# Moving two scan steps and one small product, repeating 17 scan matmuls, and five warm-ups less, in a retention and HGRN2 decoder step

## The chip, the cores and the metric

The kernel runs on one core of a Trainium2 chip. The metric is the device time of one execution in microseconds, of which there are three runs of the kernel before and one profiled execution. TensorE (PE in the profile) does the matrix products, with its weight loads shown apart as PEld; VectorE (DVE), ScalarE (ACT) and GpSimd (POOL) do the rest, and SyncE (SP) issues most transfers.

## The reference

One layer of a hybrid decoder: the normalised input is projected to eight groups of 512 columns, half of which feed four heads of retention (fixed decay by head) and half four heads of HGRN2 (a learned forget gate for each column); the gated outputs go through one output projection.

In short form:

```python
h = rmsnorm(x, norm_g)
p = (h @ w_in).astype(jnp.float32)
rq, rk, rv, rg, hq, hf, hi, hgate = jnp.split(p, 8, axis=-1)
rq, rk = rotary(rq, pos), rotary(rk, pos) * RET_DK ** -0.5
o_ret, s_ret = chunked_decay_recurrence(rq, rk, rv, log_gamma, s_ret)   # S = f*S + k v^T, o = S^T q
o_ret = head_rmsnorm(o_ret, ret_g) * silu(rg)
logf = logaddexp(log(lb), log1p(-lb) + log_sigmoid(hf))
kin = (1 - lb) * sigmoid(-hf)
o_hg, s_hg = chunked_decay_recurrence(silu(hq), kin, hi, logf, s_hg)
o_hg = head_rmsnorm(o_hg, hg_g) * silu(hgate)
y = x + concatenate([o_ret, o_hg]) @ w_out
```

It does so for a prompt of 2048 tokens of width 1024 and for eight single new tokens with states of their own (the "decode" rows). Everything is float32.

## The kernel before, in words

**Units and products.** The input projection is cut into 24 units, u = 0 to 23, in the repeating order H (HGRN2's f and q of one head), G (the gates) and R (retention's k and q of one head). Units 0 to 11 work on the first half of the prompt, 12 to 23 on the second. Eight units of the output projection follow, and the V products stand ahead of all. Each unit is a Strassen-Winograd product of seven block products; a block product is 12 matmuls of 128x512, since an operand is split into a high and a low part (names ending in h and l) in order to keep float32 accuracy. The results carry names like aG, eR, bR: the unit's kind is the second letter.

**The order.** The table AT gives nearly every piece of work a position in units of one block product, seven to a unit. Pieces are put in a heap (`at`, and `after` for a position relative to the running one) and written out in that order. The order that comes out is the order of every engine: nothing is rearranged later. The scan of the head with index u//3 gets its positions from `AT["hgrn"]` plus an offset from `AT["hd"][u // 3]`, one row of four for each of the eight scans (here counted from one: the second scan belongs to u = 3, the fourth to u = 9).

**The scan.** An HGRN2 head is scanned in steps s0 to s3, which stand between the block products of later units. Step s0 (`scores0`) makes 32 diagonal matmuls (L1287) and 32 of `small` (L1269). Steps s1 and s2 (`scores`) each make 32 calls of `small` on kept copies, tile plh<-fh,qh, and 32 on the running k and q, plh<-qth,kh. Step s3 makes 16 calls at L1321 and 16 at L1330. A float32 call is two passes on TensorE, each with a weight load, so the trace counts 64 for 32 calls. Between two steps ScalarE copies k and half of q to the kept tiles (`keep`, L1248 and L1249), VectorE multiplies running k and q by the products of the forget gates (`update`, L1234 and L1237, tiles kh and qth), and then puts the scores into place (`put`, COPY_PREDICATED). The first half of a step waits for the copies, the second for the update.

**Other names.** `dec_mm` (L809) makes the projection of the eight decode rows for unit u: 16 calls into tile pdp, from the weight tiles r6A, r6S and so on of that unit. `dec_copy` takes it off. potr is a transpose by TensorE. L750 is the addition that combines block products on VectorE (kr<-bR,kr). At the start TensorE makes 7 calls of 128x128 and `AT["wu"]` calls of 32x8 on a tile of ones (L237 and L240) before the first product.

Of the kernel before, what the change touches and what calls it, by code (L numbers as in the profile page):

```python
# [19 lines left out]
P = 128  # L20
# [6 lines left out]
CH = HALF // P  # L27
# [21 lines left out]
def spooled(u):  # L49
    return u % 3 != 1 and u % 12 != 11  # L50
# [3 lines left out]
AT = {'wvl': (0.55, 0.6, 6.2, 6.6),  # L54
 's2': (0.4, 2.6),
 'vd': (9.4, 11.2),
 'hgrn': {'s0': 12.1,
          's1': 15.8,
          's2': 17.6,
          'load': 17.5,  # L60
          's3': 19.7,
          'k': 20.9,
# [63 lines left out]
 'x1s': (0.5, 1.8, 1.9, 3.4, 5.0),  # L126
 'wo': (26.9, 71.0, 101.8, 122.8),
 'wos': (0.0, 2.3, 3.3),
 'wu': 35,
 'wop': (140.0, 2.133, 2.1, 2.833),  # L130
 'gate': {'G': 0.95, 'store': 1.6, 'R': 0.8, 'H': 0.7, 'root': 0.5, 'scale': 1.15, 'gt': 1.2, 'tr': 0.6},
 'fin': 1.0,
# [9 lines left out]
         'fin': 25.2},  # L142
 'dh': ((12.15, 14.75), (17.55, 20.15), (27.15, 28.65)),
 'dhs': (-5.0, -2.2, -2.2, -1.5),
 'hd': ((0.0, 0.0, 0.0, 0.0), (0.0, 0.0, -0.5, -0.5), (0.0, 0.0, 0.0, 0.0), (0.3, 0.0, 0.0, 0.0),
        (0.0, 0.0, 0.0, 0.0), (0.0, 0.5, 0.0, 0.0), (0.0, 0.0, 0.0, 0.0), (0.0, 0.0, 0.0, 0.5)),
 'retL': {'load': 12.0,
          's': 11.55,
# [37 lines left out]
def step_kernel(ctx, tc, a, out):  # L186
    nc = tc.nc
    pe, act, dve, pool, sp = nc.tensor, nc.scalar, nc.vector, nc.gpsimd, nc.sync
# [29 lines left out]
    def at(pos, f):  # L218
        count[0] += 1
        heapq.heappush(ev, (pos, count[0], f))  # L220

    def after(d, f):
        at(now[0] + d, f)
# [11 lines left out]
    wu = ps_tr.tile([P, P], F32, tag="tr", name="wu")  # L235
# [535 lines left out]
    def w_load(u, n):  # L771
        R[u, n] = t_get([P, GW], f"r{u}{n}")
        row, kh = {"A11": (0, 0), "S3": (1, 0), "A22": (1, 1), "A12": (0, 1)}[n]
        sp.dma_start(R[u, n].rearrange("p (k t) -> p k t", k=4), w_src(u, row, kh))

    def w_s1(u):
        R[u, "S1"] = t_get([P, GW], f"r{u}S1")
        w_add(u, "S1", "S3", "A22", ALU.add)

    def w_s3(u):  # L780
        w_add(u, "S3", "A11", "S3", ALU.subtract)

    def w_s2(u):
        R[u, "S2"] = t_get([P, GW], f"r{u}S2")
        w_add(u, "S2", "A22", "S3", ALU.subtract)

    def w_s4(u):
        R[u, "S4"] = t_get([P, GW], f"r{u}S4")
        w_add(u, "S4", "A12", "S2", ALU.subtract)

    def w_split(u, n):
        w = W[u, n] = r_get(f"w{u}{n}")
        split_raw(w, R[u, n])
        t_done(R[u, n])
        if u < 12 and spooled(u):
            after(AT["late"], lambda: pool.dma_start(w_dram[u][W_NAMES.index(n)], w.bitcast(F32)))

    def w_reload(u, n):
        w = W[u, n] = r_get(f"w{u}{n}")
        sp.dma_start(w.bitcast(F32), w_dram[u - 12][W_NAMES.index(n)])  # L800
# [3 lines left out]
    def dec_mm(u):  # L804
        dec["pt"] = ps_o.tile([P, P], F32, tag="o", name=f"pdp{u}")
        for j in range(4):
            for g, n in enumerate(("A11", "A12", "S3", "A22")):
                at_ = 32 * (4 * (g % 2) + j)
                pe.matmul(  # L809
                    dec["pt"][32 * g : 32 * g + 32], xz[:, at_ : at_ + 32], R[u, n][:, j * P : (j + 1) * P],  # L810
                    start=(j == 0), stop=(j == 3),
                )

    def dec_copy(u):
        dec["e"] = t_get([P, P], f"de{u}")
        act.activation(dec["e"], dec["pt"], AF.Copy)

    def dec_sel(u):
        pt = ps_o.tile([P, 2, NB], F32, tag="o", name=f"pds{u}")
        pe.matmul(pt, dec["e"], sel16, start=True, stop=True)  # L820
        t_done(dec["e"])
        act.activation(draw[:, u % 3, :, u // 3], pt, AF.Copy)

    def prep_events(u):
        U = 7 * u
        w, d = AT["w"], AT["dec"]
        if 12 <= u < 24 and spooled(u):
            for name in W_NAMES:
                at(U + AT["re"][name], lambda name=name: w_reload(u, name))
            return  # L830
        for n, name in enumerate(("A11", "S3", "A22", "A12")):
            at(U + {0: -7.6, 1: -8.6}.get(u, AT["w24"][0] if u == 24 else w["load"] if u % 3 or u >= 12 else w["load0"]) + 0.5 * n, lambda name=name: w_load(u, name))
        if u < 12:
            if u == 3:
                at(AT["hgrn"]["s2"] + AT["hd"][0][2] + 0.01, lambda: dec_mm(u))
            else:
                at(U + d["mm" if u % 3 or not u else "mm0"], lambda: dec_mm(u))
            at(U + (-0.65 if u < 2 else d["copy" if u % 3 else "copy0"]), lambda: dec_copy(u))
            at(U + d["sel"], lambda: dec_sel(u))
        if u == 24:  # L840
            w = dict(w, **dict(zip(("S1", "S3", "S2", "S4"), AT["w24"][1:])))
        at(U + w["S1"], lambda: w_s1(u))
        at(U + w["S3"], lambda: w_s3(u))
        at(U + w["A11"], lambda: w_split(u, "A11"))
        at(U + w["S2"], lambda: w_s2(u))
        at(U + w["sS1"], lambda: w_split(u, "S1"))
        at(U + w["S4"], lambda: w_s4(u))
        at(U + w["sS2"], lambda: w_split(u, "S2"))
        at(U + w["sS4"], lambda: w_split(u, "S4"))
        at(U + w["sA12"], lambda: w_split(u, "A12"))  # L850
        at(U + w["sS3"], lambda: w_split(u, "S3"))
        at(U + w["sA22"], lambda: w_split(u, "A22"))
# [349 lines left out]
    def hgrn_rec(u):  # L1202
        half, h = u // 12, (u % 12) // 3
        name = f"h{half}{h}"
        hd = NH + h
        d = units[u]
        f, k, q, qt = d["f"], d["k"], d["q"], d["qt"]
        box = {}

        def views(b):  # L1210
            return (
                qt.rearrange("p (n two b) -> p n two b", two=2, b=b),
                k.rearrange("p (n two b) -> p n two b", two=2, b=b),
            )
# [7 lines left out]
        def products(lo, hi):  # L1222
            if lo == 0:
                box["fp"] = s_ctx["up"].tile([P, HALF], F32, tag="fp", name=f"fp{name}")
            for li in range(lo, hi):
                two = spans(li).rearrange("p (n two) -> p n two", two=2)
                dve.tensor_tensor(spans(li + 1), two[:, :, 0], two[:, :, 1], op=ALU.mult)

        def update(li):
            b = LEVELS[li]  # L1230
            qv, kv = views(b)
            nb = HALF // (2 * b)
            two = spans(li).rearrange("p (n two) -> p n two", two=2)
            dve.tensor_tensor(  # L1234
                kv[:, :, 0, :], kv[:, :, 0, :], two[:, :, 1:2].to_broadcast([P, nb, b]), op=ALU.mult
            )
            dve.tensor_tensor(  # L1237
                qv[:, :, 1, :], qv[:, :, 1, :], two[:, :, 0:1].to_broadcast([P, nb, b]), op=ALU.mult
            )

        kept_k, kept_q = q, f[:, :512]
# [11 lines left out]
            after(0.35, copies)  # L1253
            after(1.1, lambda: update(li))

        def small(dst, li, kept=False):
            b = LEVELS[li]
            m = 32 // (2 * b)
            for c in range(CH):
                for i in range(4):  # L1260
                    at_ = c * P + 32 * i
                    if not kept:
                        kk = k[:, at_ : at_ + 32]
                        n0 = (c * 4 + i) * m
                        qq = views(b)[0][:, n0 : n0 + m, 1, :]
                    else:
                        kk = kept_k[:, at_ : at_ + 32]
                        qq = kept_q[:, at_ // 2 : at_ // 2 + 16]
                    pe.matmul(dst[32 * i : 32 * i + 32, c], kk, qq, start=True, stop=True)  # L1269

        def put(src, li):
            b = LEVELS[li]
# [8 lines left out]
        def scores0():  # L1281
            pa = ps_lv.tile([P, 2, CH, 32], F32, tag="lv", name=f"pa{name}")
            pd, p0 = pa[:, 0], pa[:, 1, :, :16]
            for c in range(CH):
                for i in range(4):
                    cc = slice(c * P + 32 * i, c * P + 32 * i + 32)
                    pe.matmul(pd[32 * i : 32 * i + 32, c], k[:, cc], q[:, cc], start=True, stop=True)  # L1287
            small(p0, 0)
            update(0)
            products(0, 1)  # L1290
            keep(1)

            def diagonal():
                products(1, len(LEVELS))
                dve.tensor_tensor(Ab, pd, id32.unsqueeze(1).to_broadcast([P, CH, 32]), op=ALU.mult)
                put(p0, 0)

            after(0.6, diagonal)

        def scores(li):  # L1300
            pl = ps_lv.tile([P, 2, CH, 16], F32, tag="lv", name=f"pl{name}{li}")
            small(pl[:, 0], li, True)
            small(pl[:, 1], li + 1)
            update(li + 1)
            keep(li + 2)

            def puts():
                put(pl[:, 0], li)
                put(pl[:, 1], li + 1)

            after(0.1, puts)
# [524 lines left out]
    for hd in range(8):  # L1836
        mm, sel = AT["dh"][hd % 3]
        p0 = 84 + 21 * (hd // 3)
# [116 lines left out]
```

## Time and profile before

| | us |
|---|---|
| median of three runs | 995.23 |
| lowest and highest | 995.17, 996.35 |
| profiled execution, its own time | 994.56 |
| its span | 992.8 |
| TensorE busy | 978.9 (99%) |
| VectorE busy | 779.6 (79%) |
| ScalarE busy | 575.5 (58%) |
| GpSimd busy | 252.5 (25%) |

The profile is of one execution. The difference between its own time and its span, 1.76 us, is what lies around the first and last recorded instruction. Busy time counts an instruction from its start to its end; TensorE's ends are modelled, and its instructions overlap, so the start times of neighbours tell better than the durations what one instruction costs. An idle time stands in brackets behind the instruction that it precedes, with what ended it; "issue" there means that nothing in the profile was waited for. Over the whole span the granted clock of TensorE is 0.999 of full speed. The DMA engines are 50 to 99% busy in most slices, since the weights, the prompt and the spooled intermediate tiles come and go all the time.

### The profile page before, as it was taken

The page shows a single profiled execution, that of the slowest core. Times are in us where ns is not written, and L with a number is a line of the kernel's source. Part 1 is how long each engine was busy: PE and PEld are TensorE (multiplying, and loading weights), DVE is VectorE, ACT ScalarE, POOL GpSimd, SP SyncE. Part 2 cuts the span into 40 slices and gives each one's busy share as a digit, 9 for nine tenths or more (in the row PEclk, how much of TensorE's full clock was granted, in tenths as well). Part 3 has the DMA queues.
Part 4 walks back from the last instruction along what each step waited for, and adds up shares of the span by engine and source line. Part 5 has one row for each costly group of instructions (what it writes and reads, how often), then busy time and mean ns, then how long its engine had stood idle before and what let it go on. Part 6 is the DMA issues. An engine that isn't in the chain of part 4 may idle for free. (4 is left out here: it accounts for less than half of the span.)

```text
span 992.8 us, 22960 instructions
## 1 busy us (share of the span) xinstructions
PE 978.9 (99%) x8831; PEld 815.9 (82%) x8831; DVE 779.6 (79%) x1355; ACT 575.5 (58%) x1348; POOL 252.5 (25%) x404
## 2 busy tenths in 40 slices
PE   9999999999999999999999999999999999999997
PEld 7788888888878887888888888888888878878886
DVE  6967696888778888878898766877867799867774
ACT  7855524856656664765885555456467577524332
POOL 1421231111332342232022222222237202312121
PEclk9999999999999999999999999999999999999999
DMA  9756669748868987784986993994996497784522
GB/s 310 239 182 245 223 218 360 291 154 301 261 194 279 300 284 266 269 273 159 354 277 187 320 307 121 317 303 130 317 333 215 156 362 275 244 267 156 212 85 85
DMA packets 121820, 244.05 MB, mean 246 GB/s; under 512 B 12600, under 2 KB 53184, under 8 KB 119024
## 3 DMA queue, kind: packets, MB, share of 16 engines
q1 hardware_dynamic: 98544, 164.69, 50.9%
q0 software_dynamic: 22880, 77.65, 21.1%
q8 instruction: 69, 1.13, 0.5%
q14 instruction: 39, 0.32, 0.1%
q10 hardware_dynamic: 288, 0.27, 0.1%
HBM read 155.97 MB, written 89.72 MB: 247 GB/s over the span
## 5 line engine op out<-in xcount | busy, mean ns | idle before, releaser
L1248 ACT ACTIVATE qh<-kh 128x1024 f32<-128x1024 f32 x24 | 25.5, 1062 | 46.3 <-DVE kh L1234 46.2
L1671 ACT ACTIVATE yj<-xro 128x512 f32<-128x512 f32 (+1 forms) x25 | 15.6, 624 | 60.3 <-DVE xro L750 42.7
L1234 DVE TENSOR_TENSOR kh<-kh,fph 128x512 f32<-128x512 f32 x48 | 33.0, 687 | 13.6 <-PE plh L1269 10.9
L1128 ACT ACTIVATE obh<-poh 128x128 f32<-128x128 f32 x64 | 16.9, 290 | 29.3 <-PE poh L1124 29.3
L1237 DVE TENSOR_TENSOR qth<-qth,fph 128x512 f32<-128x512 f32 x48 | 32.8, 683 | 0.0
L1128 ACT ACTIVATE obr<-por 128x128 f32<-128x128 f32 x64 | 16.8, 276 | 27.1 <-PE por L1124 27.1
L373 POOL TENSOR_TENSOR ms<-ms 128x2 f32<-128x2 f32 x8 | 10.0, 1255 | 86.5 <-ACT xn L369 86.5
L1689 DVE SCALAR_TENSOR_TENSOR xro<-xro,yms,fg 128x1024 f32<-128x1024 f32 (+1 forms) x16 | 20.0, 1247 | 13.5 <-POOL yms L1686 13.5
L1152 POOL DMA_DIRECT2D o_dram<-gtr x16 | 12.3, 769 | 67.5 <-DVE gtr L1149 20.8
L948 ACT ACTIVATE vo<-aV 128x512 f32<-128x512 f32 x12 | 7.1, 589 | 37.7 <-PE aV L918 37.7
L750 DVE TENSOR_TENSOR xro<-aO,xro 128x512 f32<-128x512 f32 (+1 forms) x33 | 22.2, 676 | 7.2 <-PE aO L918 7.1
L1152 POOL DMA_DIRECT2D o_dram<-gth x16 | 12.5, 778 | 57.5 <-DVE gth L1149 15.9
L265 POOL TENSOR_SCALAR orsh<-omsh 128x4 f32<-128x4 f32 x16 | 5.6, 347 | 83.3 <-ACT obh L1128 82.9
L1136 ACT ACTIVATE obh<-poh,orsh 128x128 f32<-128x128 f32 x64 | 18.2, 370 | 14.2 <-POOL orsh L266 14.2
L1115 DVE SCALAR_TENSOR_TENSOR sth<-sth,fph,puh 128x128 f32<-128x128 f32 x48 | 16.7, 347 | 10.3 <-PE poh L1124 7.8
L1122 PE MATMUL poh<-vh,A 128*128 128x128 f32 x128 | 24.0, 274 | 0.0
L1122 PE MATMUL por<-vr,A 128*128 128x128 f32 x128 | 24.0, 274 | 0.0
L1002 POOL DMA_DIRECT2D g_dram<-g x29 | 15.8, 546 | 27.8 <-DVE g L998 25.6
L1124 PE MATMUL por<-str,qr 128*128 128x128 f32 x112 | 21.8, 276 | 0.3 <-DVE str L1113 0.3
L369 ACT ACTIVATE xn<-xn 128x512 f32<-128x512 f32 x32 | 19.8, 622 | 3.5 <-DMA xn<-in_x_prompt 3.5
L1136 ACT ACTIVATE obr<-por,orsr 128x128 f32<-128x128 f32 x64 | 18.2, 368 | 6.1 <-POOL orsr L266 6.1
L1124 PE MATMUL poh<-sth,qth 128*128 128x128 f32 x112 | 21.7, 275 | 0.0
(1727 smaller groups left out, 3716.7 us busy)
## 6 DMA issues: line engine op xcount, KB each, us to landing
xn<-in_x_prompt SPq DMA_DIRECT2D x32, 256.0 KB, 4.4
v_dram<-vo SPq DMA_DIRECT2D x32, 256.0 KB, 2.4
xro<-in_x_prompt SPq DMA_DIRECT2D x16, 512.0 KB, 5.1
out_y_prompt<-xro POOLq DMA_DIRECT2D x15, 512.0 KB, 4.0
g_dram<-g POOLq DMA_DIRECT2D x29, 256.0 KB, 5.8
xr<-in_x_t SPq DMA_DIRECT2D x12, 512.0 KB, 6.2
vh<-v_dram SPq DMA_DIRECT2D x16, 256.0 KB, 8.8
gth<-g_dram SPq DMA_DIRECT2D x16, 256.0 KB, 6.7
```

The source lines that it names most:

```text
L369: act.activation(r, r, AF.Square, accum_out=ms[:, 2 * h + j : 2 * h + j + 1])
L750: dve.tensor_tensor(o, x, y, op=ALU.add)
L1115: dve.scalar_tensor_tensor(dst, src, decay(c), pu[:, j], op0=ALU.mult, op1=ALU.add)
L1122: pe.matmul(po[:, j], s_ctx["A"][:, c], box["v"][g][:, j], start=True, stop=src is None)
L1124: pe.matmul(po[:, j], qcol(c), src, start=False, stop=True)
L1128: act.activation(ob[:, j], po[:, j], AF.Square, accum_out=ms[:, j : j + 1])
L1136: act.activation(ob[:, j], po[:, j], AF.Copy, scale=rs[:, j : j + 1])
L1152: after(AT["gate"]["tr"], lambda: pool.dma_start(o_dram[c0 : c0 + 4, ty, :, h].rearrange("c p t -> p c t"), gt.rearrange("p (c t) -> p c t ...
L1234: dve.tensor_tensor(kv[:, :, 0, :], kv[:, :, 0, :], two[:, :, 1:2].to_broadcast([P, nb, b]), op=ALU.mult)
L1237: dve.tensor_tensor(qv[:, :, 1, :], qv[:, :, 1, :], two[:, :, 0:1].to_broadcast([P, nb, b]), op=ALU.mult)
L1248: act.activation(kept_k, k, AF.Copy)
L1689: dve.scalar_tensor_tensor(x[:, cc], x[:, cc], ms[:, 0:1], fg[:, cc], op0=ALU.mult, op1=ALU.mult)
```

## The change

Four edits, all to the order and to calls on TensorE:

- `wu` goes from 35 to 30 calls.
- A new table `again` makes the last part of some steps longer by repeating the first calls of the same `small` once more, into the same place with the same operands: 2 in the fourth scan's s0, 1 in its s2, 4 in the fifth's s2, 1 in the sixth's s1, 9 in the seventh's s2.
- `hd[3]`, the fourth scan: s2 one block product later, s3 0.6 later.
- The decode product of unit 6 is put right behind the second scan's s2, as that of unit 3 stood behind the first scan's already.

```diff
- 'wu': 35,
+ 'wu': 30,
+ 'again': {(3, 's0'): 2, (3, 's2'): 1, (4, 's2'): 4, (5, 's1'): 1, (6, 's2'): 9},
...
- 'hd': ((0.0, 0.0, 0.0, 0.0), (0.0, 0.0, -0.5, -0.5), (0.0, 0.0, 0.0, 0.0), (0.3, 0.0, 0.0, 0.0),
+ 'hd': ((0.0, 0.0, 0.0, 0.0), (0.0, 0.0, -0.5, -0.5), (0.0, 0.0, 0.0, 0.0), (0.3, 0.0, 1.0, 0.6),
...
-            if u == 3:
-                at(AT["hgrn"]["s2"] + AT["hd"][0][2] + 0.01, lambda: dec_mm(u))
+            if u in (3, 6):
+                at(7 * (u - 3) + AT["hgrn"]["s2"] + AT["hd"][u // 3 - 1][2] + 0.01, lambda: dec_mm(u))
...
-        def small(dst, li, kept=False):
+        def small(dst, li, kept=False, again=0):
...
-            for c in range(CH):
-                for i in range(4):
-                    at_ = c * P + 32 * i
...
+            for n in range(4 * CH + again):
+                c, i = divmod(n % (4 * CH), 4)
+                at_ = c * P + 32 * i
...
+        def more(step):
+            return AT["again"].get((u // 3, step), 0)
...
-            small(p0, 0)
+            small(p0, 0, again=more("s0"))
...
-            small(pl[:, 1], li + 1)
+            small(pl[:, 1], li + 1, again=more("s1" if li == 1 else "s2"))
```

On TensorE, the second step of the second scan before (the numbers behind the names are those of the tiles; the first column of each row is its line):

```order
L918 MATMUL aR_3234<-x0T2l,w5S_3231 128x512
L918 MATMUL aR_3234<-x0T2h,w5S_3231 128x512
L809 MATMUL pdp_3397<-r6A_3241,xz 32x128
...
L809 MATMUL pdp_3397<-r6A_3271,xz 32x128
L1269 MATMUL plh_3414<-fh_2585,qh_2625 32x16 x32
L1269 MATMUL plh_3414<-qth_2963,kh_2824 32x16 x32
L918 MATMUL aR_3234<-x0T2h,w5S_3231 128x512
```

And now:

```order
L919 MATMUL aR_3229<-x0T2l,w5S_3226 128x512
L919 MATMUL aR_3229<-x0T2h,w5S_3226 128x512
L1270 MATMUL plh_3392<-fh_2580,qh_2620 32x16 x32
L1270 MATMUL plh_3392<-qth_2958,kh_2819 32x16 x32
L810 MATMUL pdp_3459<-r6A_3236,xz 32x128
...
L810 MATMUL pdp_3459<-r6A_3266,xz 32x128
L919 MATMUL aR_3229<-x0T2h,w5S_3226 128x512
```

The 16 calls of pdp, of which the first and the last are shown, have changed places with the 64 calls of the step.

On VectorE, from the middle of the fourth scan to its end, before:

```order
L747 TENSOR_TENSOR x1B11l<-x1B11l,x1B11h 128x1024 x2
L1234 TENSOR_TENSOR kh_4983<-kh_4983,fph_5334 128x32x16
L1237 TENSOR_TENSOR qth_5117<-qth_5117,fph_5334 128x32x16
L1275 COPY_PREDICATED fh_4744<-lmask,plh_5570 128x16x8
L1275 COPY_PREDICATED fh_4744<-lmask,plh_5570 128x8x16
L750 TENSOR_TENSOR kr_5406<-eR_5419,kr_5406 128x512
L1234 TENSOR_TENSOR kh_4983<-kh_4983,fph_5334 128x16x32
L1237 TENSOR_TENSOR qth_5117<-qth_5117,fph_5334 128x16x32
L750 TENSOR_TENSOR kr_5406<-bR_5662,kr_5406 128x512
L1234 TENSOR_TENSOR kh_4983<-kh_4983,fph_5334 128x8x64
```

And now:

```order
L748 TENSOR_TENSOR x1B11l<-x1B11l,x1B11h 128x1024 x2
L751 TENSOR_TENSOR kr_5403<-eR_5416,kr_5403 128x512
L1235 TENSOR_TENSOR kh_4978<-kh_4978,fph_5331 128x32x16
L1238 TENSOR_TENSOR qth_5112<-qth_5112,fph_5331 128x32x16
L1279 COPY_PREDICATED fh_4739<-lmask,plh_5583 128x16x8
L1279 COPY_PREDICATED fh_4739<-lmask,plh_5583 128x8x16
L751 TENSOR_TENSOR kr_5403<-bR_5658,kr_5403 128x512
L1235 TENSOR_TENSOR kh_4978<-kh_4978,fph_5331 128x16x32
L1238 TENSOR_TENSOR qth_5112<-qth_5112,fph_5331 128x16x32
L748 TENSOR_TENSOR x1T1l<-x1T1l,x1T1h 128x1024
```

Both additions to kr, of eR and of bR, now stand ahead of the pair of updates (kh and qth) that they followed.

On TensorE at the fourth scan's last step, before (bR is followed at once by the step) and then now:

```order
L918 MATMUL bR_5662<-x0B21l,w11A_5511 128x512
L918 MATMUL bR_5662<-x0B21h,w11A_5511 128x512
L1321 MATMUL plh_5681<-fh_4744,qh_4783 32x32 x16
L1330 MATMUL plh_5682<-qth_5117,kh_4983 32x64 x16
L918 MATMUL aR_5391<-x0T3h,w11S_5436 128x512
L918 MATMUL aR_5391<-x0T3l,w11S_5436 128x512
```

```order
L919 MATMUL bR_5658<-x0B21h,w11A_5508 128x512
L919 MATMUL aR_5388<-x0T3h,w11S_5433 128x512
L919 MATMUL aR_5388<-x0T3l,w11S_5433 128x512
L919 MATMUL aR_5388<-x0T3h,w11S_5433 128x512 x2
L919 MATMUL aR_5388<-x0T3l,w11S_5433 128x512
L919 MATMUL aR_5388<-x0T3h,w11S_5433 128x512
L1325 MATMUL plh_5690<-fh_4739,qh_4778 32x32 x16
L1334 MATMUL plh_5691<-qth_5112,kh_4978 32x64 x16
```

Six of the twelve aR matmuls that followed the step now stand ahead of it.

## Rows read from the trace of the kernel before

**Rows 1.** The page: busy time of TensorE; the queue that brings instructions.

```profile
PE 978.9 (99%) x8831; PEld 815.9 (82%) x8831; DVE 779.6 (79%) x1355; ACT 575.5 (58%) x1348; POOL 252.5 (25%) x404
...
q8 instruction: 69, 1.13, 0.5%
```

**Rows 2.** Waits of TensorE: us in total, times, longest.

```profile
PE plh L1269 <- issue: 3.4, 2, 2.5
PE bG L918 <- issue: 1.1, 1, 1.1
```

**Rows 3.** Busy time and instruction counts by engine, between the three stalls.

```profile
290.00:394.50 104.50, 102.04 (x1274) 85.66 (x1274) 88.31 (x162) 62.83 (x149) 33.31 (x56) 1.00 0.81 270
394.50:799.50 405.00, 403.49 (x4444) 342.03 (x4443) 319.12 (x588) 254.84 (x621) 113.42 (x160) 1.00 0.77 255
```

**Rows 4.** TensorE's timeline at 288 to 292: start, us, operation, [idle before].

```profile
288.05 0.70 PE L1269 MATMUL pah<-qth,kh 128*32 128x16 f32 x62
288.68 0.50 PE L918 MATMUL bG<-x0B21h,w4A 128*128 128x512 f32 x1
290.32 0.40 PE L918 MATMUL bG<-x0B21l,w4A 128*128 128x512 f32 x1 [1.14 <-issue]
...
291.47 0.60 PE L1147 MATMUL potr<-ident,obr 128*128 128x128 f32 x4
291.82 0.48 PE L918 MATMUL aG<-x0T3h,w4S 128*128 128x512 f32 x1
```

**Rows 5.** DMA queues in 287.5:289, 392.4:393.7 and 797.3:798.5: packets, MB, share.

```profile
q8 instruction: 1, 0.02, 5.3%
...
q8 instruction: 1, 0.02, 4.9%
...
q8 instruction: 1, 0.02, 5.1%
```

**Rows 6.** TensorE's timeline at 388 to 395.

```profile
388.73 0.33 PE L809 MATMUL pdp<-r9A,xz 128*32 128x128 f32 x2
...
391.93 0.43 PE L1269 MATMUL plh<-qth,kh 128*32 128x16 f32 x31
394.81 0.44 PE L1269 MATMUL plh<-qth,kh 128*32 128x16 f32 x31 [2.46 <-issue]
```

**Rows 7.** TensorE's timeline at 790 to 800.

```profile
790.77 0.74 PE L1269 MATMUL plh<-qth,kh 128*32 128x16 f32 x64 [0.42 <-DVE qth L1237]
...
793.83 0.63 PE L918 MATMUL aG<-x1T4h,w22A 128*128 128x512 f32 x2
...
798.15 0.57 PE L1269 MATMUL plh<-qth,kh 128*32 128x16 f32 x47
799.70 0.32 PE L1269 MATMUL plh<-qth,kh 128*32 128x16 f32 x15 [0.97 <-issue]
```

**Rows 8.** TensorE's timeline at 306 to 308, second step of the second scan.

```profile
306.45 0.30 PE L809 MATMUL pdp<-r6A,xz 128*32 128x128 f32 x2
...
307.34 0.73 PE L1269 MATMUL plh<-fh,qh 128*32 128x16 f32 x62
...
307.93 0.70 PE L1269 MATMUL plh<-qth,kh 128*32 128x16 f32 x62
```

**Rows 9.** VectorE's timeline at 291 to 307.

```profile
291.67 0.69 DVE L750 TENSOR_TENSOR big<-bG,big 128x512 f32<-128x512 f32 x1 [0.37 <-PE bG L918]
...
306.25 0.68 DVE L1237 TENSOR_TENSOR qth<-qth,fph 128x512 f32<-128x512 f32 x1
```

**Rows 10.** TensorE's timeline at 482, last step of the fourth scan.

```profile
482.22 0.46 PE L1321 MATMUL plh<-fh,qh 128*32 128x32 f32 x32
482.49 0.68 PE L1330 MATMUL plh<-qth,kh 128*32 128x64 f32 x32
```

**Rows 11.** VectorE's timeline at 482.

```profile
482.32 0.69 DVE L750 TENSOR_TENSOR kr<-bR,kr 128x512 f32<-128x512 f32 x1 [0.53 <-PE bR L918]
```

**Rows 12.** TensorE's timeline at the start of the span.

```profile
4.36 0.77 PE L240 MATMUL wu<-ones 128*32 128x8 f32 x70
```

More of the change, by code (lines that the diff above doesn't have):

```diff
@@ L1254, in keep @@
             after(1.1, lambda: update(li))
-        def small(dst, li, kept=False):
+        def small(dst, li, kept=False, again=0):
             b = LEVELS[li]
             m = 32 // (2 * b)
-            for c in range(CH):
-                for i in range(4):
-                    at_ = c * P + 32 * i
[L1262 to L1269, printed above, removed]
+            for n in range(4 * CH + again):
+                c, i = divmod(n % (4 * CH), 4)
+                at_ = c * P + 32 * i
+                if not kept:
+                    kk = k[:, at_ : at_ + 32]
+                    n0 = (c * 4 + i) * m
+                    qq = views(b)[0][:, n0 : n0 + m, 1, :]
+                else:
+                    kk = kept_k[:, at_ : at_ + 32]
+                    qq = kept_q[:, at_ // 2 : at_ // 2 + 16]
+                pe.matmul(dst[32 * i : 32 * i + 32, c], kk, qq, start=True, stop=True)
+        def more(step):
+            return AT["again"].get((u // 3, step), 0)
         def put(src, li):
```

## Prediction

> **What bounds the kernel.** I read the page first. TensorE is busy for 978.9 of the 992.8 us of the span [rows 1], so what counts is what makes it stand still, and how many passes it gets. I then read the list of its waits [rows 2]. The reader is to see that the largest entries are not waits for another engine: 3.4 us in two pieces ahead of the small scan matmuls and 1.1 us ahead of a gate matmul carry the word "issue", time in which the profile shows nothing that TensorE waited for. They are three stalls: 1.14 us at 290.32 [rows 4], 2.46 us at 394.81 [rows 6], 0.97 us at 799.70 [rows 7].
>
> Their places have a pattern. TensorE's matmuls and weight loads are 2 x 8831 = 17,662, and queue q8, which brings instructions, moved 69 packets of 1.13 MB in all, some 16 KB each [rows 1]: 17,662/69 = 256 instructions for one packet. Between the first stall and the second lie 1274 matmuls and 1274 loads, 2548, between the second and the third 4444 and 4443, 8887 [rows 3]. Ten blocks of 256 are 2560 and 35 are 8960. The 12 and the 73 that are missing are TensorE's semaphore instructions there, which the profile doesn't count. So all three stalls lie at one remainder of 256: at the edge of a block of instructions.
>
> The DMA view closes the chain. One q8 packet lies in each of the stretches 287.5 to 289, 392.4 to 393.7 and 797.3 to 798.5 [rows 5], and TensorE goes on 1.1 to 1.3 us after each stretch's end (290.32, 394.81, 799.70). Hence the reading on which this forecast rests: only one block is ahead of the running one; its fetch is asked for when TensorE crosses the edge before; where the 256 instructions between are scan passes, TensorE runs through them sooner than the next block comes. The passes are short: from 307.34 to 307.93 some 64 begin, 9 ns each [rows 8], while five gate matmuls from 290.32 to 291.47 take 0.23 us each [rows 4].
>
> From edge to fetch it takes unequally long. A q8 share of 5.3% of 16 engines over 1.5 us is a packet of 1.27 us, so the first fetch begins between 287.5 and 287.7; by the same step the second begins between 392.4 and 392.7 and the third between 797.3 and 797.5. The first stall's edge before lies at the start of the 128 scan passes that end at 288.68 [rows 4]; the later 64 take 0.65 us, so it is at about 287.4: 0.3 us or less. The second stall's edge lies 128 passes before the last of the 31 passes at 391.93: 31 and 64 scan passes, six wide matmuls, and 27 of the 32 passes of pdp, so in pdp's beginning, at 388.9 [rows 6]: 3.5 us or a little more. The third's lies at 793.83 [rows 7]: 3.5 us as well.
>
> **The change part by part.** The sum is made against the profiled execution's own 994.56 us (span 992.8 and 1.76 around it). The shown median, 995.23, lies 0.67 above it; I add that at the end.
>
> 1. Five warm-up calls less are ten passes. 70 passes take 0.77 us [rows 12], so ten are 0.11 at most. The first product behind them needs a VectorE result and already waits; it would wait that much longer. Zero, bounds -0.11 and 0.
>
> 2. The 17 repeated calls are 34 passes. At 9 ns, from [rows 8], they cost 0.31; at the 11 ns of [rows 12] 0.37. I take 0.34. Nothing hides them, since TensorE is the bound.
>
> 3. First stall. The program is 20 TensorE instructions shorter ahead of it (ten passes and their loads), so the edge now falls ten matmuls later: behind the other five bG, the four potr and one aG. Without the stall the next bG comes at 290.32 - 1.14 = 289.18, potr 1.15 later, aG 0.35 after that and the edge some 0.3 behind it, at 291.0 [rows 4]. The edge before moves ten scan passes, 0.1 us, so the block is there at 290.4, 0.6 us early. -1.14, bounds -1.14 and, if the fetch is as late as the others', +2.
>
> 4. Second step of the second scan. Of the 1.14 most is given back here. Before, pdp of unit 6 stands ahead of the step from 306.45 to 307.34, and the step's second half begins at 307.90 [rows 8]. VectorE's qth, which that half reads, ends at 306.25 + 0.68 = 306.93 [rows 9], 0.97 us earlier, so it isn't waited for. In the changed order the 0.89 us of pdp are behind the step, and TensorE comes 1.14 earlier: it would be there at 307.90 - 0.89 - 1.14 = 305.87. VectorE works without a gap from 291.67 to 306.93; only the 0.37 ahead of 291.67, a wait for bG [rows 9], can go. So qth ends at 306.56 at best, with 0.05 for the signal at 306.6: a new wait of 0.74, bounds 0 and 1.1. pdp itself costs the same in either place, as do its copy and its buffer, whose orders on ScalarE don't change.
>
> 5. Second stall. The shift is still -20 there, so the edge falls ten scan passes later, in the same dense run (41 instead of 31 passes into the second half, 0.09 us), and the edge before ten pdp passes later (32 of unit 6's take 0.89 us [rows 8], so 0.3). The stall stays, between 2.46 and 2.7. I take +0.1. Outer bounds: -2.46, if the fetch begins as promptly as the first stall's, and +2.5, if its delay grows by as much as it could shrink.
>
> 6. Fourth scan. Its second step comes a product later, and twelve eR matmuls stand ahead of it; its last step comes six wide matmuls later. On VectorE the addition kr<-bR now stands ahead of the pair of updates that the last step's second half reads. Before, that addition started at 482.32, having waited for bR [rows 11], and the pair was done earlier. Now: kr<-bR at 482.32, then two updates of 0.6 each, so qth is ready at about 484.2. TensorE starts the last step six matmuls after 482.22, at 483.58, and its second half 0.27 later (482.22 to 482.49, [rows 10]), at 483.85. A wait of 0.40, bounds 0 and 0.5. The updates that are moved behind eR start when the step's passes are done, as before. No DMA is issued in another order; SP's and GpSimd's sequences are the same.
>
> 7. Third stall. Here the shift is +48 instructions, 24 passes: the edge falls 24 scan passes earlier (0.2 us), and the edge before goes from 793.83 back over 13 wide and transpose matmuls into the scan passes that run from 790.77 to 791.4 [rows 7], to about 791.3. With the same 3.5 us the fetch begins near 794.9 and the block is there by 797.3; TensorE needs it at 798.3. -0.97, bounds -0.97 and +0.2.
>
> 8. All other edges move too, by -12 to +12 instructions between the fourth scan and the seventh. No row shows how much room these blocks have. Bounds 0 and one stall like the third, 0.97; I take 0.2, an estimate.
>
> Sum: 0 + 0.34 - 1.14 + 0.74 + 0.1 + 0.40 - 0.97 + 0.2 = -0.33. From 994.56 that is 994.2, and with 0.67 for the median **994.9**.
>
> [...] The rows show stalls at block edges that end 1.1 to 1.3 us after a q8 packet [rows 4 to 7]. [...]
>
> **The rivals.**
> - The second stall goes too. For it: the first stall's fetch came within 0.3 us, so 3.5 us is no fixed price. Against it: the edge before stays inside pdp, and the same transfers surround it. With its 2.46 and the 0.1 gone: 994.9 - 2.56 = 992.3; without the waits of parts 4 and 6 as well, 991.2.
> - Slower: one moved edge makes a new large stall. Where an edge falls in a step of scan passes and the edge before it just ahead, a fetch that is 3.5 us late costs up to 2.46 us [rows 6]. For it: 35 edges lie in the 405 us between the second and the third stall [rows 3], so some 27 in the 315 us from the fourth scan to the eighth, and each gets a place that no run has shown. Against it: most of these 256 instructions are wide matmuls of 0.23 us, 128 of which are 29 us. 994.9 + 2.46 = 997.4. It decides from a delay of some 3 us on, with over 100 scan passes in one block.
> - The change doesn't do what it says: the stalls are not tied to the place in the program but to what the DMA engines do, and stay. Then only the passes and the new wait of the fourth scan count, and without the 1.14 the second scan doesn't wait (307.01 against 306.98): 994.56 + 0.34 + 0.40 + 0.67 = 996.0. Against it: the remainder of 256, three times.
>
> **How the numbers follow.** My forecast has 0.53; the second stall gone 0.18; a new large stall 0.13; stalls that stay 0.16. About 0.2%, 2 us, is what a measurement of this kernel can tell from no change, so faster means below 993.2 and slower above 997.2. The forecast's own range is 993.8 to 996.2 and holds nearly no case beyond either bound; faster comes from the first rival and a little of the forecast (0.20), slower from the second rival (0.13), the rest is 0.67. The range 992.2 to 997.5 takes in the first rival's and the second's middle; below lies 0.1, above 0.07.
>
> **What the profile after would show.** Part 3: no idle time at the gate matmul near 290, no "issue" entry for bG. Part 4: in the second scan's second step a wait of plh for VectorE's qth, about 0.7 us. Part 5: "issue" ahead of plh near 394, 2.4 to 2.7 us, ten passes further on. Part 6: a wait for qth ahead of the fourth scan's last step, 0.4. Part 7: no "issue" near 799. The forecast is wrong if "issue" entries stand at other places with over 1 us, or if the one near 394 is gone.

## The result, and the profile after

The changed kernel takes 999.52 us in the median of six executions (997.50 to 1001.16), the kernel before 995.20 beside it (993.69 to 996.35): a ratio of 1.0040, 95% interval 1.0026 to 1.0055. By the ratio it is slower by 4.0 us. The forecast was 0.3 us faster than the profiled execution and 994.9 in the median, with 997.5 as the upper end of its range. A second study of the same kernel gave 1.0039 (1.0021 to 1.0058). The profiled execution took 997.50, the fastest of the six, and its span is 995.6 us.

The page of the changed kernel has 24 TensorE passes more and one block of instructions more, against [rows 1]:

```profile
PE 981.7 (99%) x8855; PEld 817.8 (82%) x8855; DVE 780.1 (78%) x1355; ACT 576.1 (58%) x1348; POOL 248.7 (25%) x404
...
q8 instruction: 70, 1.15, 0.5%
```

TensorE is busy for 2.8 us longer and stands still as long as before. So the loss isn't in the sum of the waits: it has to be in matmuls that take longer, as well as in waits that changed places. The list of TensorE's waits, against [rows 2]:

```profile
PE plh L1270 <- issue: 2.6, 1, 2.6
PE wu L238 <- POOL ones L229: 1.1, 1, 1.1
PE plh L1270 <- DVE qth L1238: 1.0, 2, 0.6
PE pkh L1086 <- ACT A L1344: 0.9, 1, 0.9
PE aO L919 <- DVE xro L751: 0.4, 1, 0.4
PE pkh L1086 <- DVE kh L1235: 0.3, 1, 0.3
PE plh L1334 <- DVE qth L1238: 0.3, 1, 0.3
```

Of the three stalls at block edges one is left. The wait for qth in the second scan and the one at the fourth scan's last step are there as forecast. The two entries of pkh were not forecast: the one for A stands at 488.66, in the fourth scan, the one for kh at 812.2, in another scan (a profile without the moved fourth scan has it too).

The first stall is gone; the same matmul follows its neighbour after 0.33 us, where [rows 4] has 1.64 (TensorE's timeline, start and duration in us):

```profile
288.59 0.50 PE L919 MATMUL bG<-x0B21h,w4A 128*128 128x512 f32 x1
288.92 0.40 PE L919 MATMUL bG<-x0B21l,w4A 128*128 128x512 f32 x1
```

And the second scan's second step waits, where [rows 8] has none:

```profile
306.43 0.70 PE L1270 MATMUL plh<-qth,kh 128*32 128x16 f32 x62 [0.59 <-DVE qth L1238]
```

The second stall, against [rows 6], begins 41 passes into the step's second half instead of 31 and is 0.11 us longer. What stands behind it is new:

```profile
391.33 0.52 PE L1270 MATMUL plh<-qth,kh 128*32 128x16 f32 x41
394.42 0.37 PE L1270 MATMUL plh<-qth,kh 128*32 128x16 f32 x21 [2.57 <-issue]
394.72 0.64 PE L919 MATMUL eR<-x0B22h,w8S 128*128 128x512 f32 x1
395.15 0.63 PE L919 MATMUL eR<-x0B22l,w8S 128*128 128x512 f32 x1
```

From 394.72 to 395.15 one wide matmul takes 0.43 us; in [rows 4] it takes 0.23. The granted clock says why. Stretches of 2 us, busy time and count by engine (TensorE, its loads, VectorE, ScalarE, GpSimd), then granted clock, DMA share and GB/s; first the changed kernel, then the kernel before at the same place:

```profile
394.00:396.00 2.00, 1.58 (x24) 1.26 (x24) 1.15 (x2) 0.43 (x1) 1.29 (x2) 0.74 0.78 297
396.00:398.00 2.00, 2.00 (x6) 1.62 (x5) 0.65 (x3) 1.83 (x4) 0.55 (x1) 0.50 0.99 359
398.00:400.00 2.00, 2.00 (x9) 1.62 (x9) 0.56 (x1) 0.00 (x0) 0.00 (x0) 0.91 0.54 209
```

```profile
396.00:398.00 2.00, 2.00 (x10) 1.66 (x9) 1.13 (x4) 1.95 (x4) 0.84 (x2) 1.00 0.94 330
```

Six matmuls where ten stood: the clock is at 0.50 of full speed, and busy time counts the slow matmuls as work. Lost is (1 - 0.74) x 2 + 0.50 x 2 + 0.09 x 2 = 1.7 us, 3.4 us at half clock. Ahead of the fall TensorE had stood still for 2.57 us; that the wait brings the fall is not shown by this profile alone, since the kernel before waits 2.46 us here and has a granted clock of 1.00 behind it. No step of the forecast had a price for this.

At the fourth scan the last step waits for qth (0.33, forecast 0.40), and behind it pkh, the transposes of kh (L1086), wait for ScalarE:

```profile
485.52 0.65 PE L1334 MATMUL plh<-qth,kh 128*32 128x64 f32 x32 [0.33 <-DVE qth L1238]
...
488.66 1.45 PE L1086 MATMUL pkh<-ident,kh 128*128 128x128 f32 x8 [0.90 <-ACT A L1344]
```

ScalarE's timeline there, changed kernel first, then before:

```profile
484.17 2.01 ACT L744 ACTIVATE x1T1h<-x1T1l 128x1024 fp32r<-128x1024 f32 x2
486.20 0.63 ACT L1010 ACTIVATE big<-kr 64x512 f32<-64x512 f32 x1
486.84 0.63 ACT L1011 ACTIVATE big<-kr 64x512 f32<-64x512 f32 x1
487.50 1.10 ACT L1344 ACTIVATE A<-plh 32x128 f32<-32x128 f32 x4
```

```profile
481.93 1.06 ACT L743 ACTIVATE x1T1h<-x1T1l 128x1024 fp32r<-128x1024 f32 x1
482.89 1.09 ACT L1340 ACTIVATE A<-plh 32x128 f32<-32x128 f32 x4
...
486.38 1.06 ACT L743 ACTIVATE x1T1h<-x1T1l 128x1024 fp32r<-128x1024 f32 x1
487.47 0.63 ACT L1009 ACTIVATE big<-kr 64x512 f32<-64x512 f32 x1
```

The A copies, which take the last step's scores off, now stand behind a second x1T1h copy and the pair big<-kr, some 2.3 us of work that stood behind them before. They begin at 487.50, and pkh begins at 488.66. Matched matmul by matmul with the kernel before, TensorE falls back 0.5 us at the last step and 1.5 at pkh, 2.0 in all.

The third stall, [rows 7], is gone: the step runs through without a wait.

```profile
801.64 0.70 PE L1270 MATMUL plh<-qth,kh 128*32 128x16 f32 x62
```

For this one execution the sum is then -1.14 + 0.59 + 0.11 + 1.7 + 0.5 + 1.5 - 0.97 + 0.34 = 2.6 of the 2.94 us between 997.50 and 994.56; the 0.34 for the repeats is the forecast's. Another 0.2 lies at the start, where the matmuls behind the fewer warm-ups come that much later. The median lies 2 us above this execution, so something happens in others that it doesn't show.

### The profile page after: what moved, and what is told of

It reads as the page before. It is cut to its first block, busy times and chain, and to the rows that moved or that the text cites. A ratio compares the mean times of both kernels' runs of the same rounds, so it can differ in the third digit from the quotient of the medians.

```text
span 995.6 us, 23007 instructions
## 1 busy us (share of the span) xinstructions
PE 981.7 (99%) x8855; PEld 817.8 (82%) x8855; DVE 780.1 (78%) x1355; ACT 576.1 (58%) x1348; POOL 248.7 (25%) x404
## 5 line engine op out<-in xcount | busy, mean ns | idle before, releaser
L374 POOL TENSOR_TENSOR ms<-ms 128x2 f32<-128x2 f32 x8 | 5.7, 718 | 88.6 <-ACT xn L370 88.6
```

## The experiments

Each study ran its kernels beside the kernel before on one chip; the studies are from several chips, so the ratios are compared, not the times. Of the kernel before there are 98 executions from the first four studies: the 65 with a granted clock of 0.998 or more (mean over the execution) have a median of 995.2 us, the 33 below it 997.8. So to tell a difference of 0.2% between two kernels takes several executions of each.

**The stall at 394 and the clock.** The first experiment takes the decode product of unit 9 from ahead of the third scan's step to behind it. Theory A, which the expectations name from here on, has the clock fall in the wake of the second stall, so that the fall goes where the stall goes; for this kernel, with both gone, it had 997.5 - 2.6 - 1.7 = 993.2.

```diff
-            if u in (3, 6):
+            if u in (3, 6, 9):
```

> The changed kernel with the decode product of unit 9 also put behind its step (third scan). [...] Rival B (the clock falls for another reason than the stall): the stall goes, the clock still falls somewhere, 994.9, granted clock 0.997. Rival C (the fetch comes when the transfers of queue q0 near 392 are over, whatever the edge): the stall stays, 997.5.

Measured: 1.0033 (1.0017 to 1.0050); the profiled execution took 1000.15. The stall grew, and moved into pdp:

```profile
396.37 0.37 PE L810 MATMUL pdp<-r9A,xz 128*32 128x128 f32 x1 [3.44 <-issue]
```

Theory A had the edge wrong: it was to lie some 23 wide matmuls ahead of the step. The stalls of the kernel before lie 2560 and 8960 instructions apart, 10 and 35 times 256, and the author takes an edge to lie at a fixed count from the start of the program. With pdp's 64 instructions taken from ahead of the step, the step slid forward into the block, and the edge came to lie nine passes into the step: the block now holds 119 scan passes and nine of pdp and no wide matmul at all. TensorE ran through it in 1.6 us of work, where the changed kernel's block took 3.3, and stalled for 3.44. So rival C (the fetch comes whenever the transfers allow) isn't needed, though its place fits; the clock fell again, from 0.1 us ahead of the stall's end on, for as long as in the changed kernel (0.56 of full speed in 396 to 398 and 0.59 in 398 to 400).

**The fourth scan.** The changed kernel with `hd[3]` back at `(0.3, 0.0, 0.0, 0.0)`, run twice; the kernel before with `(0.3, 0.0, 1.0, 0.6)` alone; and one execution of it with `(0.3, 0.0, 1.0, 0.0)`.

```diff
- 'hd': ((0.0, 0.0, 0.0, 0.0), (0.0, 0.0, -0.5, -0.5), (0.0, 0.0, 0.0, 0.0), (0.3, 0.0, 1.0, 0.6),
+ 'hd': ((0.0, 0.0, 0.0, 0.0), (0.0, 0.0, -0.5, -0.5), (0.0, 0.0, 0.0, 0.0), (0.3, 0.0, 0.0, 0.0),
```

> The changed kernel with the fourth scan's steps back at their old positions. Theory A: the waits of the fourth scan's last step (0.4) and of the transposes pkh behind it (1.6 us of drift) go, the second stall and the clock's fall stay: 2.0 us faster than the changed kernel, 995.5 against its profiled 997.5. Rival D (the moved steps carry the whole loss): as the kernel before, 4 us faster than the changed kernel.

> The changed kernel with the fourth scan's steps at their old positions, as once before (995.75 in the median of ten, ratio 1.0004), for a narrower interval. Theory A: the moved steps cost the changed kernel 2.0 us and the moved block edges the other 1.6 to 2.0: ratio to before 1.0015 to 1.002. Rival D (the moved steps carry the whole loss): ratio 1.000 again.

> The kernel before with only the fourth scan's steps moved (second step 1.0, last step 0.6 products later). Theory A: 2.0 us slower than before, with waits of pkh for ScalarE's A copies and of the last step for qth; the three stalls stay at 290, 394 and 799. Rival D: 4 us slower.

> The kernel before with only the fourth scan's second step a product later, its last step at the old place. If the wait of the transposes pkh for ScalarE's A copies (0.9 us) comes from the last step's 0.6 alone, it is gone here, and the last step waits for qth or the kept copies for about 1 us instead, since only one product lies between the two steps; if it comes from the second step's move, it stays.

Measured: without the move 1.0004 (0.9985 to 1.0022) and 1.0008 (0.9989 to 1.0027); the move alone 1.0020 (1.0007 to 1.0033). The profile of the move alone has the two waits of the fourth scan, beside the old three stalls:

```profile
PE pkh L1086 <- ACT A L1344: 0.9, 1, 0.9
...
PE plh L1334 <- DVE qth L1238: 0.3, 1, 0.3
```

With the last step left at its old place pkh's wait for A is gone and the last step waits instead:

```profile
PE plh L1334 <- DVE qth L1238: 1.7, 1, 1.7
```

So the moved steps cost 2.0 us by themselves, the size of the two drifts in the profile. Matched with the kernel before, TensorE falls back 1.9 us at the fourth scan with both steps moved and 1.8 with the second step alone (one execution each): the second step's move is enough for the whole cost, and the last step's 0.6 decides which wait takes it.

Inside the changed kernel the move is worth more: 1.0040 against 1.0006, the mean of the two without it, is 3.4 us, give or take 1.7. This is nearer to rival D than to theory A. Part of it is the clock: the mean granted clock is 0.9963 over 13 executions of the changed kernel, 0.9974 over the 22 without the move and 0.9978 over the 98 of the kernel before, and 0.0011 of 996 us is 1.1 us. Why the clock falls less often without the move is open, and so is whether 2.0 and 3.4 differ at all.

**Two moves combined**: the changed kernel with unit 9's product behind its step, unit 6's ahead again, and the old fourth scan.

```diff
-            if u in (3, 6):
+            if u in (3, 9):
```

> The changed kernel with unit 9's decode product behind its step, unit 6's back ahead of its step, and the fourth scan at its old positions; repeats and warm-ups as changed. Theory A: no stall at a block edge over 1 us, no fall of the clock, no new wait: before's profiled 994.56 less 1.14, 2.46 and 0.97, plus 0.34 for the repeats: 990.3. Rival B: 992. Rival C: 993.

Measured: 1.0000 (0.9981 to 1.0019). The expected 990.3 was a miss, for the first one's reason: the stall near 394 was 2.75 us in pdp, with the clock's fall to 0.50 behind it. And a stall was there that neither the kernel before's nor the changed kernel's profile had shown, 1.6 us at 226.5, in the first scan's second step; the first experiment's profile has it too (1.93 at 226.82).

**The changed kernel once more.**

> The changed kernel once more, unchanged, for more times with their granted clocks and a second profile. [...]

Measured: 1000.12 in the median of seven, where theory A had 999.3; the profiled execution took 1002.18. It has the stall near 394 with 2.51 us (at 399.54, since all comes later), but no fall of the clock behind it: 1.00 in every stretch from 400 to 440. The fall lies behind an earlier stall that the first profile didn't have, so theory A's place for it was wrong here (TensorE's timeline, then a stretch of 2 us):

```profile
224.60 0.58 PE L1270 MATMUL plh<-qth,kh 128*32 128x16 f32 x49
227.34 0.28 PE L1270 MATMUL plh<-qth,kh 128*32 128x16 f32 x11 [2.16 <-issue]
```

```profile
228.00:230.00 2.00, 2.00 (x26) 1.52 (x18) 1.50 (x4) 1.57 (x3) 0.00 (x0) 0.50 1.02 320
```

It lies at a block edge, and the block is one that the five warm-ups less have shortened: before, TensorE took from 217.85 to 224.08 for it, 6.2 us; in the first profile of the changed kernel from 220.57 to 224.79, 4.2 us, since ten wide matmuls went out of it at the front and ten passes came in at the back. In that profile its fetch began at 222.15 and landed at 223.07, just in time; here it began at 224.91. Of the ten profiles with 30 warm-ups five have this stall, of 1.6 to 2.2 us; of the five with 35 to 39 none has it. If the other executions are like the profiled ones, about half of them lose some 2 us there, and 1.7 more where the clock falls; the ten profiles are too few to say it closer.

**Repeats moved.** As many repeats, elsewhere; then the same idea in the old order.

```diff
- 'again': {(3, 's0'): 2, (3, 's2'): 1, (4, 's2'): 4, (5, 's1'): 1, (6, 's2'): 9},
+ 'again': {(2, 's1'): 9, (3, 's2'): 4, (6, 's2'): 4},
```

> The changed kernel with the same number of repeats, 17, put elsewhere: 9 behind the third scan's first step, 4 behind the fourth's second, 4 behind the seventh's second. The block edge near 394 then falls 36 instructions earlier than in the changed kernel, and the block ahead of it gets 36 instructions of wide matmuls for passes. Theory A: the second stall goes to 0.3 us or less (-2.3) and the clock's fall with it (-1.6): 995.3 in the median against the changed kernel's 999.3, granted clock 0.998 to 0.999. Rival B: the stall goes, the clocks stay at 0.996 to 0.997: 997.0. Rival C (the fetch comes when the transfers allow, whatever the edge): 999.3.

Measured: 1.0012 (0.9995 to 1.0028), against 1.0039 for the unmoved kernel in the same study. The profiled execution took 994.17 and has no wait at any block edge:

```profile
PE wu L238 <- POOL ones L229: 1.1, 1, 1.1
PE pkh L1086 <- ACT A L1344: 0.9, 1, 0.9
PE plh L1270 <- DVE qth L1238: 0.8, 2, 0.4
```

Its granted clock is 1.00 in every stretch until 987, by when the matmuls have ended. The kernel does the same work in the same order with the same number of passes, and only the count of instructions ahead of each place differs. But part of this is luck. The block ahead of the edge near 394 took 4.4 us, where the changed kernel's took 3.3 without its stall, so that the moved edge is worth some 1.0 of the 2.57. The rest is an early fetch: it began at 388.76, 0.7 us behind the edge before (388.09), and in the changed kernel's profile at 392.10, 3.6 us behind (388.54). The queue that brings instructions, in 388.5 to 390 of this profile and then in 391.8 to 393.3 of the changed kernel's:

```profile
q8 instruction: 1, 0.02, 4.3%
```

```profile
q8 instruction: 1, 0.02, 4.2%
```

By the times, 0.27% apart with intervals that overlap, the gain is likely but not clear.

> The kernel before (fourth scan and unit 6's decode product at their old places) with 30 warm-ups and 13 repeats: 9 behind the third scan's first step, 4 behind the fourth's second. Theory A: none of the three stalls over 0.3 us, no new wait and no fall of the clock: the median of before, 995.7, less 1.1, 2.3 and 0.9, plus 0.2 for the repeats, and less some 1 for the executions in which before loses its clock: 991. Rival B: 992.5. Rival C: 994.

The edit, beside `hd[3]` and unit 6 as before:

```diff
- 'again': {(3, 's0'): 2, (3, 's2'): 1, (4, 's2'): 4, (5, 's1'): 1, (6, 's2'): 9},
+ 'again': {(2, 's1'): 9, (3, 's2'): 4},
```

Measured: 1.0011 (0.9997 to 1.0025), a miss. In the profiled execution the stall at 227.4 is there (1.66), and the one near 394 too, 2.26, with the clock's fall (its last stretch, 400 to 400.5, at 0.90), though the kernel ahead, with the same repeats up to there, had none. Its block took 4.0 us without the stall, about as long, but the fetch began 3.9 us behind the edge and not 0.7. So of these two edges, with 4.4 and 4.0 us of work in the block ahead, one has no wait and one has 2.26 us of it, and the start of the fetch is what differs.

**Only the warm-ups.**

```diff
- 'wu': 35,
+ 'wu': 30,
```

> The kernel before with 30 warm-up calls instead of 35, nothing else: 20 TensorE instructions less ahead of everything, no work moved. Theory E (what counts is where the block edges fall): the stall at 290 goes (-1.1); edges at other steps fall worse, since the wide matmuls in their blocks give way to passes: stalls of 2 to 3 us each near 630 and 710, where before has none, the one at 394 stays, and one of about 2 near 225 in part of the executions: 4 us slower than before (2 to 6). Rival F (the stalls belong to the DMA traffic and not to the place in the program): 0.1 us faster, within noise, and issue waits where before has them.

Measured: 1.0044 (1.0025 to 1.0064), 1000.57 in the median of twelve. Leaving out ten passes whose results nothing reads makes the kernel 4.4 us slower. Rival F is out: the stall at 290 is gone, as theory E said. Of the other places that were named, 394 stalled in the profiled execution (2.46), and 225, 630 and 710 did not; the largest stall was at 801, where the edge had moved to the end of the step:

```profile
797.51 0.65 PE L1270 MATMUL plh<-qth,kh 128*32 128x16 f32 x57
801.11 0.25 PE L1270 MATMUL plh<-qth,kh 128*32 128x16 f32 x5 [2.95 <-issue]
```

```profile
802.00:804.00 2.00, 2.00 (x8) 1.52 (x7) 1.21 (x4) 1.87 (x3) 0.00 (x0) 0.61 1.13 358
```

The terms -1.14 at 290, 2.95 instead of 0.97 at 801 and 1.7 for the half clock make 2.5 of the 3.0 us by which this execution is slower than the profiled one before.

There is a rival: warm-ups could also set how soon TensorE is at full speed. In all ten profiles with 30 of them no stall of 0.5 us or more stands near 290, and in all five with 35 to 39 there is one of 1.1 to 2.1, which no slow start explains. But one of the ten, of the changed kernel without the moved scan, does start slowly: its first matmuls come 0.43 us apart, the spacing of the half-clock stretch behind 394, and its matmuls are 1.8 us behind those of the kernel before for the next 140 us.

```profile
9.62 0.63 PE L500 MATMUL pv<-B12h,x0B11h 128*128 128x512 f32 x1
10.05 0.63 PE L500 MATMUL pv<-B12l,x0B11h 128*128 128x512 f32 x1
...
10.80 0.39 PE L500 MATMUL pv<-wvT4h,x0B21h 128*128 128x512 f32 x1
11.02 0.39 PE L500 MATMUL pv<-wvT4l,x0B21h 128*128 128x512 f32 x1
```

The granted clock of the profile reads 1.00 there too, so this is read from the spacing alone. In the profile with only the warm-ups changed the start is worth 0.35 us. So the slow start adds some tenths of a microsecond, once in ten profiles 1.8, and not 4.4.

Against the changed kernel without its moved scan (1.0004 and 1.0008), which has the same 30 warm-ups, the repeats and the move of unit 6's product together are worth some 3.8 us, nearly all of what the five warm-ups less cost; that compares studies on different chips, with an interval of 2.3 us to either side.

**Searches for a faster version**, by counting how long TensorE takes for the block ahead of each edge and taking the fetch delays from the traces. The first is the changed kernel with unit 9's product at a place of its own and the old fourth scan, the other two are the kernel before with other warm-ups:

```diff
- 'again': {(3, 's0'): 2, (3, 's2'): 1, (4, 's2'): 4, (5, 's1'): 1, (6, 's2'): 9},
+ 'again': {(1, 's1'): 1, (1, 's2'): 3, (2, 's0'): 2, (2, 's1'): 3, (4, 's0'): 4},
...
-            if u in (3, 6):
+            if u == 9:
+                at(U - 2.3, lambda: dec_mm(u))
+            elif u in (3,):
```

```diff
- 'wu': 35,
+ 'wu': 39,
```

```diff
- 'wu': 35,
+ 'wu': 38,
+ 'again': {(4, 's0'): 4},
```

> The kernel before with 30 warm-ups, 13 repeats (1 and 3 behind the second scan's s1 and s2, 2 and 3 behind the third's s0 and s1, 4 behind the fifth's s0) and the decode product of unit 9 one and a half products behind the third scan's second step instead of ahead of it. Theory E: no stall at 290, none over 0.5 us at 394, since the block there holds 25 wide matmuls; the one near 225 in part of the executions remains: 2 to 3 us faster than before, 993.5. Rival F: as before, 996.

> The kernel before with 39 warm-up calls instead of 35, nothing else: the block edges fall 16 instructions earlier in the program everywhere, so that the block ahead of the edge near 394 holds 8 more wide matmuls. Theory E: the stall near 394 goes to some 0.4 us and with it the clock's fall there; the one near 290 stays at 1.2 to 1.5, the one near 800 goes to 0.2: 2.5 to 3.5 us faster than before, ratio 0.997. Rival F (the edges don't matter): 0.1 slower at most, ratio 1.000, 2.4 us of wait near 394.

> The kernel before with 38 warm-ups and 4 repeats behind the fifth scan's s0. Theory E: as with 39 warm-ups up to 500 us (the stall near 394 at 0.4 to 0.8), and more room at the edges near 545 than there: 3 us faster than before, ratio 0.997. Rival F: ratio 1.000.

Measured: 1.0027 (1.0006 to 1.0049), 1.0002 (0.9987 to 1.0018) and 1.0016 (1.0000 to 1.0033). None is faster than before. The first one's profile has stalls of 2.18, 0.52 and 3.56 us, at 227, 393 and 399, where none over 0.5 was expected at 394. With 39 warm-ups the stall near 394 shrank, but to 1.64 and not to 0.4, and the one near 290 grew:

```profile
PE pah L1270 <- issue: 2.1, 1, 2.1
PE plh L1270 <- issue: 1.6, 1, 1.6
```

The delays of a few profiles don't tell those of other executions well enough to place 70 edges by them.

## Why the prediction was wrong

Its reading of the stalls was right about their place and about the fetch behind each, and both carried over to 15 profiles. With TensorE's semaphore instructions counted in (12 between the first two stalls of the kernel before, 73 between the second and the third), all 30 stalls marked issue of 0.5 us and more lie at one remainder of 256, and each ends 1.2 to 1.6 us after the landing of a fetch that began 0.2 to 4.2 us after the edge before. What the traces don't show is when a fetch is asked for. In the profiles before and after there are 69 and 70 packets and as many edges; a packet begins from 5.2 us ahead of the edge with its number to 6.7 behind it, and TensorE gets past the next edge 1.26 us after the packet's landing at the soonest. Of 70 edges a profile has none to three that cost 0.5 us or more.

Point by point, by its parts:

- Parts 1 and 2 (warm-ups and repeats as passes): nearly right. Part 1's zero left out the start: with fewer warm-ups the first matmuls came later, by 0.24 us from 20 us on. The fifth scan's four repeats cost 0.1, as priced. As counts both were worth far more, which is part 8.
- Part 3 (first stall, -1.14): right, and gone in all ten profiles with 30 warm-ups.
- Part 4 (wait in the second scan, 0.74): 0.59. The 0.05 for the signal holds: the matmul at 306.43 begins 0.05 behind the end of qth.
- Part 5 (second stall stays, +0.1): the wait was right, 0.11 longer. What was missing is its wake: the clock at 0.50 of full speed, for 1.7 us of lost time. It was not in the sum nor among the bounds, since before's second stall, 2.46, had no such wake in its trace.
- Part 6 (fourth scan, 0.40, at most 0.5): the step that failed most clearly. Its wait was right (0.33), but it was taken for the whole. The x1T1h and kr copies on ScalarE now stand ahead of the A copies, and pkh behind them came 1.5 later, so that the fourth scan costs 2.0. The move alone measured 2.0 too, and taking it out of the changed kernel gave back 3.4. Part 6 followed the last step's wait for VectorE and no further; the order on ScalarE would have shown the rest.
- Part 7 (third stall, -0.97): right, in the profiled execution.
- Part 8 (all other edges, 0.2, up to 0.97): mis-sized. It named the edges from the fourth scan to the seventh, and the one that cost lies ahead of them: at 225 a block lost 2 us of its work, and the edge behind it stalls for 1.6 to 2.2 in five of ten profiles; with the clock behind it that is up to 3.9 in one execution.

An estimate puts the median together from these. To the forecast's -0.33 come 1.6 for the fourth scan (2.0 instead of 0.40), 1.5 for the clock (0.9963 against 0.9978 of 996 us), and 0.9 for the edge at 225 (half of the profiles, 1.9 each) instead of 0.2: 3.5 of the 4.0. Without the moved scan, that is without part 6 altogether and with the clock at 0.9974, the same terms give 0.4, where 0.6 was measured. It was the second rival, a moved edge with a new large stall, that came true in half of the profiles, and its 997.4 was too low, as it had neither the clock nor pkh.

That the clock's fall belongs to the stalls is shown by place: in 15 profiles there are ten falls, each of which begins between 1.0 us ahead of the end of a stall of 1.8 us or more and 1.3 us behind it, and none elsewhere until the last matmul. Which stalls have one is open: 19 are that long, nine of them have none (2.46 in the kernel before, 2.81 in one without the moved scan), and none of the eleven shorter ones has.

## What to carry to other kernels

In this kernel, which TensorE bounds to 99%, an idle "issue" wait of 2.57 us had 1.7 us of lost clock behind it: look at the granted clock right behind such a wait. Where hundreds of small matmuls follow each other, count the instructions: here those left out or added ahead moved the block edges behind them (30 stalls at one remainder of 256), and ten passes less, with nothing else changed, cost 4.4 us. And when a step is moved in an order written by hand, read the order of every engine at that place: the wait that was forecast was on VectorE (0.5 us behind at the last step), the one that cost three times as much on ScalarE (1.5 at pkh).

## What the runs showed that was not expected

Ten warm-up passes, 0.11 us of work, are worth 4.4 us (1.0044), of which the later start of the first matmuls is some tenths and the rest goes with the count of instructions.

The block edge near 225 was neither safe nor unsafe by itself. The same block of the changed kernel, 4.2 us long, was in time in one execution (fetch at 222.15) and 2.16 us late in another (224.91). This is one reason why this kernel's times spread: the changed kernel's 13 executions run from 997.3 to 1002.2.

In nine of the ten falls the clock stayed at half equally long, 3.4 us, which costs up to 1.7 us; in one it stayed twice as long, 6.8 us, from 1.0 us ahead of the end of a stall of 3.56 on, and cost 2.9.
